# Attention weights copied into float32r tiles before they are transposed

## The chip, the cores and the metric

The kernel runs on one core of a Trainium2 chip. Its matmuls run on TensorE (PE in the profile; PEld is the same engine loading the stationary operand), the rest on VectorE (DVE), ScalarE (ACT) and GpSimd (POOL); SyncE (SP) issues most transfers. The metric is the device time of the run in microseconds; lower is better.

## The reference

One layer of a hybrid encoder, 1024 tokens by 1024 features, all in float32. The input is normalised and modulated, projected, and split over 16 heads of 64 features. Eight heads do softmax attention with a forget gate, eight do stick-breaking attention. Each head's output is gated, all are projected back, and a residual with a second normalisation ends the layer.

```python
# forgetting attention (8 heads)
s = einsum('bhqd,bhkd->bhqk', q, k) * scale + (f_q[..., :, None] - f_k[..., None, :])
p = softmax(where(causal, s, -inf));          out = einsum('bhqk,bhkd->bhqd', p, v)
# stick-breaking attention (8 heads)
log_keep = where(strict, log_sigmoid(-z), 0); later = cumsum(log_keep, reverse=True) - log_keep
w = where(strict, exp(log_sigmoid(z) + later), 0);  out = einsum('bhqk,bhkd->bhqd', w, v)
```

## The kernel before, in words

**Number formats.** float32r is TensorE's faster form of float32 with fewer mantissa bits. To keep precision, most operands are split into a rounded part (hi) and the rest (lo), both float32r, and a product is three matmuls (L312, L313, L314 for the projections). The transposes of the attention weights are different: they take the weights in plain float32 with a float32 identity.

**Units.** Heads go in pairs p = 0 to 7: pairs 0 to 3 are stick-breaking, 4 to 7 forgetting. A unit (p, h, i) is one block of 128 queries (i = 0 to 7) of head h of pair p; it sees ke = (i + 1) x 128 keys. There are 128 units, 16 to a pair. Pairs 1 to 3 run i upward, pairs 4 to 6 downward. Units are counted by k: pair 2 is k = 32 to 47, pair 4 is 64 to 79, pair 5 is 80 to 95, pair 6 is 96 to 111.

**A unit's steps.** att_scores: TensorE's scores (L483, L484) into PSUM. For stick-breaking, ACT's two sigmoids (L506, L508), DVE's scans (L514, L518) and POOL's product (L520) with its last column set to zero (L521) leave the weights in a tile be. For forgetting, DVE's addition and minimum (L491), ACT's exponential (L496), a reciprocal and POOL's scaling (L499) leave them in a tile a. Both come from one pool, att, of six tiles. att_transpose: i + 1 transposes of 128 x 128 (L537) into PSUM tiles T of up to four blocks, from each of which ACT writes the rounded part (L539) and DVE the rest (L540). A transpose is a matmul whose stationary operand is the block and whose moving operand is the identity. When both units of a pair of query blocks are transposed, att_pv multiplies by the values (L554).

**Order.** TensorE's order is written by hand: the loop at the end takes k = 0 to 130, and in each step issues the scores of unit k, the transposes of unit k - LAG (LAG = 2), and a share of the filling work from `fill`, which is the projections of later pairs, the values and the output. The other engines' and SP's orders are set by the scheduler, from the dependences and its own idea of times; each engine then runs its list strictly in order, so an instruction that waits holds all that follow on its engine.

**Value tiles.** The tag v is a pool of three 8 KB-per-partition buffers for the value tiles of a pair (two pairs are made at a time by make_v), and, at the two ends of the kernel, for the modulation's weights and for the last normalisation's gain and bias (load_ln, L905 and L906).

**Transfers.** SP issues the weight fetches (L123), whose results POOL splits (L125, L127, L128) into a ring of five tiles, the stores of gated outputs (L578), of scaled output weights (L896, L897), the copies of the keys from one half of the partitions to the other (L298), and the loads of the output weights (L886, L887). ACT issues the loads of the forget rows fb (L443).

Of the kernel before, what the change touches and what calls it, by code (L numbers as in the profile page):

```python
# [27 lines left out]
def tile_hybrid_layer(  # L28
# [55 lines left out]
    def after(*instructions):  # L84
        stack = ExitStack()
        for i in instructions:
            stack.enter_context(tc.issue_after(i.ins))
        return stack


    ident = cp.tile([P, P], F32, tag="ident", name="ident")
    make_identity(nc, ident)
    causal = cp.tile([P, P], F32, tag="causal", name="causal")
    nc.gpsimd.memset(causal, 0.0)
    nc.gpsimd.affine_select(out=causal, in_=causal, pattern=[[-1, P]], base=0,
                            channel_multiplier=1, compare_op=ALU.is_ge, fill=MASKED)
# [354 lines left out]
    def att_query(u):  # L451
# [3 lines left out]
        r = slice(h * HD, h * HD + HD)  # L455
        nc.scalar.copy(z[r, :], qst[p][h].bitcast(F32)[r, i * P:i * P + P])  # L456

    masks, scaled, lows, gates = [], [], [], []

    def att_causal(u):  # L460
# [9 lines left out]
    def att_scores(u, following):  # L470
        p, h, i = u
        z = zq.pop(u)
        ke = (i + 1) * P
        ns = 1 if ke <= 512 else 2
        w = ke // ns
        qs = slice(i * P, i * P + P)
        if p >= 4:
            f = fb[2 * (p - 4) + h]
        S = s_tile(f"S_{p}_{h}_{i}")
        halves = range(ns) if p >= 4 else range(ns)[::-1]  # L480
        for s in halves:
            ks = slice(s * w, s * w + w)
            nc.tensor.matmul(S[:, s, :w], qst[p][h][:, qs], kst[p][h][:, ks], start=True, stop=False)  # L483
            nc.tensor.matmul(S[:, s, :w], z, klo[p][:, ks], start=False, stop=True)  # L484
        v3 = lambda a: a[:, :ke].rearrange("p (a b) -> p a b", a=ns)
        if p >= 4:
            a = att_tile(f"a_{p}_{h}_{i}")
            nm = sb.tile([P, 1], F32, tag="nm", bufs=4, name=f"nm_{p}_{h}_{i}")
            l = sb.tile([P, 1], F32, tag="l", bufs=4, name=f"l_{p}_{h}_{i}")
            with after(*lows):  # L490
                nc.vector.tensor_tensor_reduce(out=v3(a), in0=S[:, :ns, :w], in1=v3(f),  # L491
                                               op0=ALU.add, op1=ALU.min, scale=-1.0, scalar=BIG,
                                               accum_out=nm)
            if following:
                att_causal(following)
            nc.scalar.activation(a[:, :ke], a[:, :ke], AF.Exp, scale=-1.0, bias=nm, accum_out=l)  # L496
            nc.vector.reciprocal(l, l)  # L497
            scaled[:] = [*scaled[-3:],
                         nc.gpsimd.tensor_scalar(a[:, :ke], a[:, :ke], l, 1.0, op0=ALU.mult, op1=ALU.mult)]  # L499
            st_w[u] = a  # L500
        else:
            kp = att_tile(f"kp_{p}_{h}_{i}")
            be = att_tile(f"be_{p}_{h}_{i}")
            with after(*key_casts):
                for s in halves:
                    nc.scalar.activation(kp[:, s * w:s * w + w], S[:, s, :w], AF.Sigmoid, scale=-1.0)  # L506
            key_casts.clear()
            last_act = nc.scalar.activation(v3(be), S[:, :ns, :w], AF.Sigmoid)  # L508
            gates[:] = [last_act]


            lo = ke - w
            rv = kp[:, lo:ke][:, ::-1]
            last_dve = nc.vector.tensor_tensor_scan(rv, rv, floor[:, :ke - lo], initial=0.0,  # L514
                                                    op0=ALU.mult, op1=ALU.max)
            if lo:
                rv = kp[:, :lo][:, ::-1]
                last_dve = nc.vector.tensor_tensor_scan(rv, rv, floor[:, P:P + 1].to_broadcast([P, lo]),  # L518
                                                        initial=kp[:, lo:lo + 1], op0=ALU.mult, op1=ALU.max)
            nc.gpsimd.tensor_tensor(be[:, :ke - 1], be[:, :ke - 1], kp[:, 1:ke], op=ALU.mult)  # L520
            nc.gpsimd.memset(be[:, ke - 1:ke], 0.0)  # L521
            st_w[u] = be
            return last_act, last_dve

    def att_transpose(u, between=()):
        p, h, i = u
        a = st_w.pop(u)
        j, qo = i // 2, (i % 2) * P
        for g in range((i // 4) + 1):
            n = min(4, i + 1 - 4 * g)  # L530
            if (p, h, j, g) not in st_pt:
                st_pt[p, h, j, g] = pt_tile(f"pt_{p}_{h}_{j}_{g}", F32R, [P, 2, 4, 256])
            hi, lo = (st_pt[p, h, j, g][:, x] for x in range(2))
            tp = t_tile(f"T_{p}_{h}_{i}_{g}")
            for b in range(n):
                kb = 4 * g + b
                nc.tensor.transpose(tp[:, b * P:(b + 1) * P], a[:, kb * P:(kb + 1) * P], ident)  # L537
            t3 = tp[:, :n * P].rearrange("p (a b) -> p a b", a=n)
            nc.scalar.copy(hi[:, :n, qo:qo + P], t3)  # L539
            lows[:] = [nc.vector.tensor_tensor(lo[:, :n, qo:qo + P], t3, hi.bitcast(F32)[:, :n, qo:qo + P],  # L540
                                               op=ALU.subtract)]
            while between:
                att_pv(*between.pop(0))
# [292 lines left out]
    for kb in range(NB):  # L836
# [9 lines left out]
        if kb < len(evacs):  # L846
            n, h = evacs[kb]
# [194 lines left out]
    FILL = (52, 72, 68, 68, 72, 72, 58, 16)  # L1042
    LEAD = 2
    LAG = 2
    W0 = 100.0
    OUT0 = 4
    TAIL = (2, 2, 2, 2, 2, 2, 4, 4, 4, 4, 8)
# [6 lines left out]
    def fill(want):  # L1054
        while done[0] < want:
            done[0] += 1
            next(fillers, None)
# [25 lines left out]
    tail = chain([gen_out_first(6), gen_out_last(6)] + [gen_out(t) for t in OUT_ORDER[1:]])  # L1083
    fill(4)
    def weights_turn(k):
        if LAG <= k < len(units) + LAG:
            u = units[k - LAG]
            att_transpose(u, ready)
            seen.add(u)
            if (u[0], u[1], u[2] ^ 1) in seen:  # L1090
                ready.append((u[0], u[1], u[2] // 2))
        while k >= len(units) + LAG and ready:
            att_pv(*ready.pop(0))

    def scores_turn(k):
        if k < len(units):
            if k == 16 * 4 - 1:
                load_fb(0)
                load_fb(1)
            if k == 0:  # L1100
                att_query(units[0])
            issued = att_scores(units[k], units[k + 1] if k + 1 < len(units) else None)
            if k == 16 * 4 - 1:
                att_causal(units[k + 1])
            if k in HELD:
                m, h = HELD[k]
                with after(*issued):
                    evac_m(0, m, 1, held[:, m * 512:(m + 1) * 512], (h,))
            with after(*(issued or ())):
                while summed:  # L1110
                    att_sum(*summed.pop(0))
            if k + 1 < len(units):
                att_query(units[k + 1])
            p, h, i = units[k]
            if 4 <= p < NPAIR - 1 and i == 0:
                load_fb(2 * (p - 4) + h + 2)

    for k in range(len(units) + LAG + 1):
        if k < 16 * 4:
            weights_turn(k)  # L1120
            scores_turn(k)
        else:
            scores_turn(k)
            fill(want[2 * k + LEAD + 1])
            weights_turn(k)
        fill(want[2 * k + LEAD + 2])
        if k >= LAST + OUT0:
            for _ in range(TAIL[min(k - LAST - OUT0, len(TAIL) - 1)]):
                next(tail, None)
        if k == LAST:  # L1130
# [69 lines left out]
```

## Time and profile before

| | |
|---|---|
| median of 3 runs | 680.5 us (680.24 to 680.56) |
| the profiled execution, first to last instruction (span; the page gives no other time for it) | 678.6 us |
| TensorE busy | 668.3 us, 98% |
| DVE, POOL, ACT busy | 72%, 60%, 56% |
| transposes of the weights (L537) | 576, 89.4 us of record time |
| transfers | 81.55 MB, mean 120 GB/s |

A row of the grouped view reads: line, engine, operation, what it writes and reads, shapes, count, then busy us and mean ns of one, then the idle time of the engine just before and what ended it. A matmul's duration goes from its start until its result is out, and neighbours overlap; what one costs TensorE is the distance from its start to the next one's. A row of the timeline starts with the start time and the duration in us; "x4" is four instructions in a row.

### The profile page before, as it was taken

Reading aid. Unit: us, or ns where it says so; the run is one execution under the profiler, and the core shown is the slowest. Engines: PE = TensorE matmul, PEld = TensorE weight load, DVE = VectorE, ACT = ScalarE, POOL = GpSimd, SP = SyncE. Lnnn points to the kernel's source line nnn. Section 1 sums busy time; section 2 is a strip of 40 time slices with the busy share of each in tenths; the row PEclk is TensorE's granted clock in tenths of the full one; section 3 lists DMA queues with packets and bytes.
Section 4 is the critical chain, followed back from the end, with each engine's and each line's share of the span. In section 5 each row is a group of like instructions: output and inputs, shape, how many; then the busy total and the mean of one; then the engine's idle time right before and its main releaser. Section 6 shows DMA issues by size and latency. Waiting matters only on the chain.

```text
span 678.6 us, 11231 instructions
## 1 busy us (share of the span) xinstructions
PE 668.3 (98%) x3713; PEld 571.2 (84%) x3713; DVE 485.9 (72%) x1001; ACT 382.6 (56%) x889; POOL 405.2 (60%) x530
## 2 busy tenths in 40 slices
PE   8999999999999999999999999999999999999995
PEld 4888898888998888889988888889988888888885
DVE  6787779868677777686776675766676777775645
ACT  5576468757567667576675564655565766521000
POOL 5560279755357556556378878785785365655412
PEclk9999999999999999999999999999999999999998
DMA  9983432112101112122124555263452297153301
GB/s 326 401 312 126 139 79 75 41 28 67 29 20 56 54 42 57 40 54 56 49 93 144 151 164 174 87 201 112 127 169 59 70 350 302 59 177 107 120 32 63
DMA packets 46474, 81.55 MB, mean 120 GB/s; under 512 B 5264, under 2 KB 20176, under 8 KB 46416
## 3 DMA queue, kind: packets, MB, share of 16 engines
q1 hardware_dynamic: 44832, 76.37, 35.1%
q10 hardware_dynamic: 1584, 4.47, 2.1%
q8 instruction: 29, 0.48, 0.3%
q14 instruction: 29, 0.24, 0.1%
HBM read 60.34 MB, written 16.29 MB: 113 GB/s over the span
## 4 chain that ended last, share of the span: by engine, by line
PE 97%; DMA 1%; DVE 0%; POOL 0%; ACT 0%; issue 0%; SPq 0%; POOLq 0%
PE m L312 11%; PE m L314 10%; PE m L313 10%; PE pv L554 10%; PE T L537 9%; PE S L484 5%; PE S L483 5%; PE o L939 4%; PE o L937 4%; PE o L938 4%; PE v L370 4%; PE v L372 4%; PE v L371 4%; PE st_q L647 1%; PE st_k L647 1%; PE st_late L647 1%
## 5 line engine op out<-in xcount | busy, mean ns | idle before, releaser
L540 DVE TENSOR_TENSOR pt<-T,pt 128x512 fp32r<-128x512 f32 (+2 forms) x192 | 102.7, 553 | 43.8 <-ACT pt L539 42.2
L539 ACT CAST pt<-T 128x512 fp32r<-128x512 f32 (+2 forms) x192 | 88.9, 479 | 64.5 <-PE T L537 62.5
L312 PE MATMUL m<-uh,whi 128*128 128x512 f32 x304 | 123.3, 405 | 0.1
L314 PE MATMUL m<-uh,wlo 128*128 128x512 f32 x304 | 119.8, 394 | 0.0
L313 PE MATMUL m<-ul,whi 128*128 128x512 f32 x304 | 119.7, 394 | 0.0
L520 POOL TENSOR_TENSOR be<-be,kp 128x127 f32<-128x127 f32 (+3 forms) x64 | 78.9, 1234 | 36.2 <-DVE kp L518 24.4
L554 PE MATMUL pv<-pt,v 128*128 128x512 f32 x320 | 82.8, 388 | 0.0
L514 DVE TENSOR_TENSOR_SCAN kp<-kp,floor 128x128 f32<-128x128 f32 (+3 forms) x64 | 58.6, 915 | 17.6 <-ACT kp L506 17.4
L499 POOL TENSOR_SCALAR a<-a,l 128x1024 f32<-128x1024 f32 (+3 forms) x64 | 48.4, 756 | 34.3 <-DVE l L497 26.0
L483 PE MATMUL S<-k,q 128*128 128x512 f32 (+5 forms) x192 | 68.8, 360 | 0.0
L314 PEld LDWEIGHTS m<-uh,wlo 128*128 128x128 f32 x304 | 57.1, 188 | 13.7
L496 ACT ACTIVATE a<-a,nm 128x1024 f32<-128x1024 f32 (+3 forms) x64 | 49.8, 779 | 28.6 <-DVE nm L491 28.1
L312 PEld LDWEIGHTS m<-uh,whi 128*128 128x128 f32 x304 | 57.2, 188 | 10.2 <-PE T L537 0.3
L484 PE MATMUL S<-kl,qz 128*128 128x512 f32 (+5 forms) x192 | 65.2, 341 | 0.0
L313 PEld LDWEIGHTS m<-ul,whi 128*128 128x128 f32 x304 | 57.3, 188 | 9.0
L554 PEld LDWEIGHTS pv<-pt,v 128*128 128x128 f32 x320 | 55.5, 189 | 8.9
L570 POOL TENSOR_TENSOR ty<-ty,sg 64x256 f32<-64x256 f32 x64 | 46.9, 733 | 23.4 <-issue 12.2
L491 DVE CUSTOM_DVE_ANT_0 a<-S,fb 128x1024 f32<-128x1024 f32 (+3 forms) x64 | 48.2, 753 | 16.9 <-PE S L484 12.0
L456 ACT CAST qz<-q 64x128 fp32r<-64x128 f32 x128 | 37.3, 296 | 34.2 <-PE S L484 33.0
L506 ACT ACTIVATE kp<-S 128x384 f32<-128x384 f32 (+4 forms) x96 | 44.0, 494 | 21.5 <-PE S L484 20.2
L370 PE MATMUL v<-whi_v,uh 128*128 128x256 f32 (+1 forms) x192 | 54.7, 285 | 0.0
L372 PE MATMUL v<-wlo_v,uh 128*128 128x256 f32 (+1 forms) x192 | 54.2, 282 | 0.0
(296 smaller groups left out, 1628.3 us busy)
## 6 DMA issues: line engine op xcount, KB each, us to landing
raw<-in_w_qkg_dram SPq DMA_DIRECT2D x38, 256.0 KB, 2.7
wss<-in_w_ss_dram SPq DMA_DIRECT2D x14, 512.0 KB, 8.1
x<-in_x_dram SPq DMA_DIRECT2D x8, 512.0 KB, 7.1
k<-k SPq DMA_DIRECT2D x32, 128.0 KB, 2.3
wg<-in_w_gate_dram SPq DMA_DIRECT2D x8, 512.0 KB, 4.9
raw_o<-in_w_out_dram SPq DMA_DIRECT2D x16, 256.0 KB, 3.0
fb<-f_dr ACTq DMA_DIRECT2D x8, 512.0 KB, 4.5
wo_dr<-whi_o SPq DMA_DIRECT2D x16, 256.0 KB, 2.1
```

What stands on the lines that cost most here:

```text
L312: nc.tensor.matmul(acc, hi[:, c], u_hi[kt][:, s], start=(kt == 0), stop=False)
L313: nc.tensor.matmul(acc, hi[:, c], u_lo[kt][:, s], start=False, stop=False)
L314: nc.tensor.matmul(acc, lo[:, c], u_hi[kt][:, s], start=False, stop=(kt == NB - 1))
L370: nc.tensor.matmul(acc[:, :n], u_hi[kt][:, ts_], hi[:, s], start=(kt == 0), stop=False)
L372: nc.tensor.matmul(acc[:, :n], u_hi[kt][:, ts_], lo[:, s], start=False, stop=(kt == NB - 1))
L483: nc.tensor.matmul(S[:, s, :w], qst[p][h][:, qs], kst[p][h][:, ks], start=True, stop=False)
L484: nc.tensor.matmul(S[:, s, :w], z, klo[p][:, ks], start=False, stop=True)
L520: nc.gpsimd.tensor_tensor(be[:, :ke - 1], be[:, :ke - 1], kp[:, 1:ke], op=ALU.mult)
L537: nc.tensor.transpose(tp[:, b * P:(b + 1) * P], a[:, kb * P:(kb + 1) * P], ident)
L539: nc.scalar.copy(hi[:, :n, qo:qo + P], t3)
L540: lows[:] = [nc.vector.tensor_tensor(lo[:, :n, qo:qo + P], t3, hi.bitcast(F32)[:, :n, qo:qo + P], op=ALU.subtract)]
L554: nc.tensor.matmul(acc2[:, :, q0:], vt[p][:, kb, h * P:(h + 1) * P], pt[:, :, q0:], start=(kb == 0), stop=(kb == last))
```

## The change

The identity is now a float32r tile with a float32 view of the same bytes. A new function hop, called when a unit's weights are ready, looks whether the unit's number lies in HOPS (35 to 47, 66 to 83, 98 to 111) and whether it has more than 256 keys. If so, it takes one half of a "room", a float32r tile of two times 1024 columns in the third buffer of the tag v (one room for each of the three ranges), and puts a transfer on a list that copies the weights there, byte for byte. The two halves are used in turn. send issues the listed transfers on SP: for pairs 0 to 3 one unit later than the unit's scores, just before the next unit's scores; for pairs 4 to 7 after the transposes that follow the unit's scores. att_transpose then transposes the copy as float32r, with the float32r identity, into the same PSUM tile. Units of other numbers go as before. The copied units are 35: eleven in pair 2, ten in pair 4, four in pair 5, ten in pair 6.

For units 32 to 48 (LATE) the transposes come three units after the scores and not two; at the end of the range two units are transposed in one step.

```diff
+    ident_r = cp.tile([P, P], F32R, tag="ident", name="ident")
+    ident = ident_r.bitcast(F32)
+    nc.gpsimd.memset(ident, 0.0)
+    nc.gpsimd.affine_select(out=ident_r, in_=ident, compare_op=ALU.not_equal, fill=1.0, base=0,
+                            pattern=[[-1, P]], channel_multiplier=1)
...
+    def hop(u, w, ke):
+        n = next((n for n, (a, b) in enumerate(HOPS) if a <= units.index(u) < b), None)
+        if n is None or ke <= 2 * P:
+            return w
+        if n not in room:
+            room[n] = sb.tile([P, 2, SEQ], F32R, tag="v", bufs=3, name=f"w_room_{n}")
+        hops[0] += 1
+        to = room[n][:, hops[0] % 2]
+        k = units.index(u)
+        late = u[0] < 4 or any(a <= k < b for a, b in LATE)
+        unsent.append((k + late, to.bitcast(F32)[:, :ke], w[:, :ke]))
+        return to
+
+    def send(k):
+        while unsent and unsent[0][0] <= k:
+            nc.sync.dma_start(*unsent.pop(0)[1:])
...
-            st_w[u] = a
+            st_w[u] = hop(u, a, ke)
...
-            st_w[u] = be
+            st_w[u] = hop(u, be, ke)
...
+        hopped = a.dtype == F32R
...
-                nc.tensor.transpose(tp[:, b * P:(b + 1) * P], a[:, kb * P:(kb + 1) * P], ident)
+                if hopped:
+                    nc.tensor.transpose(tp.bitcast(F32R)[:, b * P:(b + 1) * P], a[:, kb * P:(kb + 1) * P], ident_r)
+                else:
+                    nc.tensor.transpose(tp[:, b * P:(b + 1) * P], a[:, kb * P:(kb + 1) * P], ident)
...
+    HOPS = ((35, 48), (66, 84), (98, 112))
+    LATE = ((32, 49),)
...
-        if LAG <= k < len(units) + LAG:
-            u = units[k - LAG]
+        for n in (LAG + 1, LAG):
+            if not 0 <= k - n < len(units) or (n > LAG) != any(a <= k - n < b for a, b in LATE):
+                continue
+            u = units[k - n]
             att_transpose(u, ready)
...
             weights_turn(k)
+            send(k)
             scores_turn(k)
         else:
             scores_turn(k)
             fill(want[2 * k + LEAD + 1])
             weights_turn(k)
+            send(k)
```

Three places show the new order. The first is TensorE's list in pair 2, head 0, between two projection groups of pair 4's queries (fcum belongs to the forget gate). T_h_i_g is the PSUM tile of group g of unit i of head h, S its scores. Before, the unit ahead of the scores of i = 6 is i = 4, from its tile be:

```order
L427 MATMUL fcum<-flf,fscratch 128x64
L428 MATMUL fcum<-fsb,ones 128x64
L537 MATMUL T_0_4_0_2730<-ident,be_0_4_2652 128x128 x4
L554 MATMUL pv_0_1_2737<-pt_0_1_0_2636,v_1955 128x512 x3
L554 MATMUL pv_0_1_2737<-pt_0_1_0_2636,v_1955 128x2x128
L537 MATMUL T_0_4_1_2743<-ident,be_0_4_2652 128x128
L483 MATMUL S_0_6_2747<-k_0_1747,q_0_1564 128x448
```

Now, at the same place:

```order
L429 MATMUL fcum<-flf,fscratch 128x64
L430 MATMUL fcum<-fsb,ones 128x64
L563 MATMUL T_0_3_0_2725<-ident,w_room_2612 128x128 x4
L507 MATMUL S_0_6_2733<-k_0_1747,q_0_1564 128x448
L508 MATMUL S_0_6_2733<-kl_1749,qz_80 128x448
```

Unit i = 3 now stands ahead of the scores of i = 6, from the room; i = 4 and the multiplication by the values have moved behind one unit's filling work. In pairs 4 to 6 the order of the matmuls is as before.

The second is SP's list at the start of pair 5, whose first unit is (5, 0, 7). Before:

```order
L123 DMA raw_1_1_5111<-in_w_qkg_dram 128x512
L123 DMA raw_o_1_5117<-in_w_out_dram 128x512
L578 DMA y_dr<-ty_1_1_4952 64x256
L123 DMA raw_o_0_5240<-in_w_out_dram 128x512
L896 DMA wo_dr<-whi_o_1_5120 128x512
L897 DMA wo_dr<-wlo_o_1_5121 128x512
L123 DMA raw_v_0_5317<-in_w_v_dram 128x512
```

Now:

```order
L125 DMA raw_1_1_5138<-in_w_qkg_dram 128x512
L125 DMA raw_o_1_5144<-in_w_out_dram 128x512
L606 DMA y_dr<-ty_1_1_4975 64x256
L480 DMA w_room_4207<-a_0_7_4949 128x1024
L480 DMA w_room_4207<-a_0_6_4996 128x896
L125 DMA raw_o_0_5267<-in_w_out_dram 128x512
L924 DMA wo_dr<-whi_o_1_5147 128x512
L480 DMA w_room_4207<-a_0_5_5040 128x768
L925 DMA wo_dr<-wlo_o_1_5148 128x512
L125 DMA raw_v_0_5344<-in_w_v_dram 128x512
```

The copies stand between the fetches of weights and the stores, which keep their order among themselves.

The third is SP's list at the end of pair 6, where the loads of the last normalisation's gain and bias (lngb) now come, behind all copies and right ahead of the output weights (wol, woh):

```order
L480 DMA w_room_5981<-a_1_2_6475 128x384
L942 DMA yr_4_6652<-y_dr 128x3x128
L942 DMA yr_0_6937<-y_dr 128x4x128
L300 DMA k_0_6318<-k_0_6318 64x512
L977 DMA xr_7207<-in_x_dram 128x1024
L942 DMA yr_4_6943<-y_dr 128x3x128
L300 DMA k_1_6319<-k_1_6319 64x512
L933 DMA lngb<-in_ln_g_dram 128x1024
L934 DMA lngb<-in_ln_b_dram 128x1024
L915 DMA wol_6586<-wo_dr 128x1024
L914 DMA woh_6585<-wo_dr 128x1024
```

Before, the two loads stood among the weight fetches of pair 6's first units.

More of the change, by code (lines that the diff above doesn't have):

```diff
@@ L5 @@
 from concourse import mybir
-from concourse.masks import make_identity
 from concourse._compat import with_exitstack
@@ L88, in after @@
         return stack
-    ident = cp.tile([P, P], F32, tag="ident", name="ident")
-    make_identity(nc, ident)
+    ident_r = cp.tile([P, P], F32R, tag="ident", name="ident")
[3 more added lines that the diff above has]
+                            pattern=[[-1, P]], channel_multiplier=1)
     causal = cp.tile([P, P], F32, tag="causal", name="causal")
@@ L456, in att_query @@
         nc.scalar.copy(z[r, :], qst[p][h].bitcast(F32)[r, i * P:i * P + P])
+    hops = [0]
+    room, unsent = {}, []
+    def hop(u, w, ke):
[13 more added lines that the diff above has]
+            nc.sync.dma_start(*unsent.pop(0)[1:])
     masks, scaled, lows, gates = [], [], [], []
```

## Prediction

> **What bounds the kernel now.** I read the first and fourth parts of the page (busy time, the chain that ended last), then the waits of TensorE.
>
> ```profile
> span 678.6 us, 11231 instructions
> PE 668.3 (98%) x3713; PEld 571.2 (84%) x3713; DVE 485.9 (72%) x1001; ACT 382.6 (56%) x889; POOL 405.2 (60%) x530
> PE 97%; DMA 1%; DVE 0%; POOL 0%; ACT 0%; issue 0%; SPq 0%; POOLq 0%
> ...
> PE sc_all L179 <- POOL ident masks.py:199: 1.5, 1, 1.5
> PE xT_early L256 <- ACT x L222: 0.9, 1, 0.9
> PE st_q L647 <- ACT uh L270: 0.4, 1, 0.4
> ```
>
> The chain is TensorE for 97% of the span, and TensorE's listed waits come to 2.8 us, all in the start phase (x, modulation, first projection). So during attention a nanosecond taken out of TensorE's stream shortens the run by a nanosecond, and a wait put into it lengthens the run by as much. The other engines have room (DVE, the fullest, is busy 72%).
>
> **What a transpose costs.** The next rows are groups of TensorE's matmuls and weight loads (busy us, mean ns of one), then two stretches of its timeline (start, duration in us).
>
> ```profile
> L537 PE MATMUL T<-ident,be 128*128 128x128 f32 x288 | 44.7, 273 | 0.0
> L537 PE MATMUL T<-ident,a 128*128 128x128 f32 x288 | 44.7, 272 | 0.0
> L537 PEld LDWEIGHTS T<-ident,a x288: 137/140/143, 355.6 to 617.5; 128*128 128x128 f32 x144
> L434 PEld LDWEIGHTS frow<-ident,fc x1: 109/109/109, 234.9 to 234.9; 128*64 128x64 f32 x1
> L314 PEld LDWEIGHTS m<-uh,wlo 128*128 128x128 f32 x304 | 57.1, 188 | 13.7
> ...
> 405.16 0.40 PE L314 MATMUL m<-uh,wlo 128*128 128x512 f32 x1
> 405.39 0.71 PE L537 MATMUL T<-ident,a 128*128 128x128 f32 x5
> ...
> 377.34 0.22 PE L483 MATMUL S<-k,q 128*128 128x128 f32 x1
> 377.40 0.27 PE L484 MATMUL S<-kl,qz 128*128 128x128 f32 x1
> 377.51 0.45 PE L312 MATMUL m<-uh,whi 128*128 128x512 f32 x1
> 377.80 0.39 PE L313 MATMUL m<-ul,whi 128*128 128x512 f32 x1
> ```
>
> Five transposes last 0.71 us together, one 0.27: they follow each other every (0.71 - 0.27)/4 = 0.11 us. No float32r transpose stands in this trace. The nearest row is the 128-column score matmul, which is float32r: 0.22 us against 0.27, so its columns stream in 0.05 us less (about 0.055 against 0.11). But a transpose has its block as the stationary operand, so each needs a load, and a stream of 0.055 us helps only if the next load is as short. Loads first: in transposes 64 columns take 109 ns and 128 take 140, so 128 columns cost about 2 x 31 = 62 ns of loading (an estimate from these two rows) and the rest is latency. The projection's float32r loads take 188, 48 more, so about 110 ns of loading. The last four rows show what that does: from the first narrow matmul to the second wide one pass 377.80 - 377.34 = 0.46 us; a wide one streams in 405.39 - 405.16 = 0.23, so the narrow ones cost 0.115 each, though one streams in 0.055. They wait for loads.
>
> So two prices bound the new transpose. If its load is that of the float32 transpose (62 ns), it follows its neighbour after about 0.06 us and saves 0.05; if its load is that of a float32r matmul (110 ns), it saves nothing. I take the first: the plain float32 matmuls at the start also load in the long time (the row below, 190 ns), as float32r does, so the short load goes with the transpose and not with the number format, while the short stream goes with float32r.
>
> ```profile
> L185 PEld LDWEIGHTS sc_all<-ident,sc x16: 190/190/192, 6.1 to 8.1; 128*128 128x128 f32 x16
> ```
>
> The last transpose of a group is followed by a float32r matmul whose own long load can only begin with it, so that one keeps its 0.11 us. The Trainium skill, "TensorE: Matmul & The Clock Gate", section "LDWEIGHTS (loading the stationary operand)", has a load cost its columns over 1.2 GHz, 107 ns for 128, whatever the format; by that rule the sum of the next part would lose its gain entirely. The 188 and 190 ns rows fit the rule, the 140 and 109 ns rows of the transposes do not.
>
> **The change part by part.**
>
> *Transposes.* 35 units are copied; they have 191 of the 576 transposes, in 47 uninterrupted groups by the order. 191 - 47 = 144 transposes save 0.05 us: **-7.2 us**. If the last of each group saved too it would be 191 x 0.05 = 9.6.
>
> *Copies.* 35 transfers are added on SP's queue, 128 rows of 4 x ke bytes: 192 to 512 KB. The trace has no copy of this size from the on-chip memory to itself. Nearest rows (KB each, median us from issue to landing; the last row has the key copies' least, median and most):
>
> ```profile
> k<-k SPq DMA_DIRECT2D x32, 128.0 KB, 2.3
> fb<-f_dr ACTq DMA_DIRECT2D x8, 512.0 KB, 4.5
> wo_dr<-whi_o SPq DMA_DIRECT2D x16, 256.0 KB, 2.1
> xr<-in_x_dram SPq DMA_DIRECT2D x8, 512.0 KB, 3.5
> out_dram<-r SPq DMA_DIRECT2D x2, 512.0 KB, 2.8
> ...
> DMA to landing us min/median/max: 2.2/2.3/4.9
> ```
>
> 512 KB lies between 2.8 (a write) and 4.5 (a broadcast read). I take 3.3, near the plain read of 3.5, and 0.2 less for each 64 KB less, which gives 2.5 for 256 KB. What hides a copy is the time between the end of POOL's last write of the weights (L499 in pairs 4 to 7, L520 and L521 in pairs 0 to 3) and the unit's first transpose. A transpose whose copy is late holds all of TensorE, since everything behind it waits in its queue. I set the two ends beside each other for every copied unit. For most of pairs 4 to 6 there are 4 to 8 us. The thin ones, POOL's row first and TensorE's second:
>
> ```profile
> 242.85 2.00 POOL L520 TENSOR_TENSOR be<-be,kp 128x1023 f32<-128x1023 f32 x1 [1.52 <-DVE kp L518]
> 245.31 1.04 PE L537 MATMUL T<-ident,be 128*128 128x128 f32 x8
> 249.21 0.27 PE L537 MATMUL T<-ident,be 128*128 128x128 f32 x1
> 422.88 1.12 POOL L499 TENSOR_SCALAR a<-a,l 128x1024 f32<-128x1024 f32 x1
> 426.63 0.60 PE L537 MATMUL T<-ident,a 128*128 128x128 f32 x4
> 499.52 0.93 POOL L499 TENSOR_SCALAR a<-a,l 128x768 f32<-128x768 f32 x1
> 503.06 0.60 PE L537 MATMUL T<-ident,a 128*128 128x128 f32 x4
> 508.50 0.69 POOL L499 TENSOR_SCALAR a<-a,l 128x512 f32<-128x512 f32 x1
> 510.78 0.49 PE L537 MATMUL T<-ident,a 128*128 128x128 f32 x3
> 520.52 1.13 POOL L499 TENSOR_SCALAR a<-a,l 128x1024 f32<-128x1024 f32 x1 [0.36 <-DVE l L497]
> 525.03 0.60 PE L537 MATMUL T<-ident,a 128*128 128x128 f32 x4
> 525.88 1.02 POOL L499 TENSOR_SCALAR a<-a,l 128x896 f32<-128x896 f32 x1 [1.09 <-DVE l L497]
> 529.62 0.60 PE L537 MATMUL T<-ident,a 128*128 128x128 f32 x4
> ```
>
> Pair 2: the longest unit of head 0 (first three rows) leaves 0.46 us today, not enough for any copy. LATE moves its transposes to the next unit's place, 249.21, which leaves 4.4; the copy needs 3.3, and the two units before it are shortened by some 0.5: covered. Without LATE TensorE would wait about 3 us there.
>
> Pairs 5 and 6 keep LAG = 2. Each deficit is copy + 0.1 for the hand-over + what the transposes of the two units before it save - the space. Unit (5,0,7): 3.3 + 0.1 + 0 - 2.6 = 0.8. Unit (6,0,5): 2.9 + 0.1 + 0 - 2.6 = 0.4. Unit (6,0,3): 2.5 + 0.1 + 0.4 - 1.6 = 1.4, but part of its lateness goes (next). Unit (6,1,7): 3.3 + 0.1 - 3.4 = 0. Unit (6,1,6): 3.1 + 0.1 + 0.3 - 2.7 = 0.8.
>
> *The normalisation's gain and bias.* Their two 512 KB loads now wait for the buffer that the third room holds, and move behind pair 6's copies. Today they are issued at 496.3 us, and POOL then waits for a weight transfer that shared the engines with them:
>
> ```profile
> L905 SPq DMA_DIRECT2D lngb<-in_ln_g_dram x1: 525/525/525, 496.3 to 496.3; - x1
> ...
> 504.55 0.62 POOL L127 TENSOR_SCALAR whi<-raw 128x512 fp32r<-128x512 f32 x1 [1.12 <-DMA raw<-in_w_qkg_dram]
> ```
>
> That 1.1 us stands ahead of unit (6,0,3)'s scaling, whose deficit so falls to about 0.2 (0.3 rounding up). Later they go out just ahead of the output weights' 16 loads; the first output matmuls read only two of the eight pairs, and I take the rest to have room: 0.
>
> *Other SP work.* Each copy waits on SP for POOL (and for the transposes of the unit two before, which used the same half); weight fetches, y stores and key copies queue behind it. They wait for the same POOL stream today and stand in POOL's order beside the copies, so I cost this at 0; if that cover is gone, a fetch a few us late meets the ring of five weight tiles, which hides it.
>
> *Order.* In pair 2 ACT's and DVE's evacuations move by one unit with the transposes; nothing is added to them. POOL's identity is built by the same two instructions.
>
> **Sum:** -7.2 + 0.8 + 0.4 + 0.3 + 0 + 0.8 = **-4.9 us**. The profiled span of 678.6 becomes 673.7. The median of the runs, 680.5, is 1.9 above the span; the same 1.9 gives **675.6 us**.
>
> **The rivals.**
>
> *A, copies never late* (each lands within the space): the whole 7.2 stays, 673.3. For it: the writes above take 2.1 to 2.8 us, and a unit that is late gives the next one room. Against it: 1.6 to 2.7 us of space at four units.
>
> *B, the load sets the pace* (110 ns, as for float32r matmuls): no transpose gets faster, TensorE streams as today, and the late copies are pure loss: 0.8 + 0.4 + 0.5 (unit (6,1,6), now without the shortening) = 1.7, so 682.2, slower. It decides at one row: the float32r transpose's load at 188 instead of 140. For it: every float32r load of the trace has 188. Against it: the float32 matmuls have 190 too. This is the case in which the skill's rule above holds.
>
> *C, slow copies*: on-chip copies of 512 KB run like the 4.5 us broadcast, 1.2 us more each. Then the five thin units pay up to 2.0 + 1.6 + 1.5 + 1.2 + 2.0, and the next thinnest about 2 together: 10.3 against 7.2, so 683.6. The turn is at about 0.6 us over my price. For it: with other transfers in flight even the 128 KB key copies reach 4.9. Against it: their median is 2.3.
>
> **How the numbers follow.** Forecast 52%, A 24%, B 16%, C 8%. Runs of this kernel agree within 0.3 us, and I call up to 0.2% (1.4 us) no change. The forecast's own range is 673 to 679; nearly all of it and all of A is faster. Between the cases (half the gain eaten by waits) lies some "same". Faster 0.74, same 0.07, slower 0.19. The range starts below A, for the case that the groups' last transposes also gain, and ends between the forecast's edge and B: 672 to 681.5.
>
> **What would show it.** Float32r transposes spaced 0.06 us, loads near 140 ns: step one holds; spaced 0.11 us: B. Copies of 512 KB landing after about 3.3 us, and TensorE waits on them at (5,0,7), (6,0,5), (6,1,6) of under 1 us each and none in pair 2. Waits at many units, or a 512 KB copy over 4 us, would be C. The forecast is wrong as a whole if TensorE's share of the chain falls well below 97%.

## The result, and the profile after

The changed kernel takes 682.93 us (median of 10 runs, 680.29 to 684.04) against 680.45 (10 runs, 680.07 to 680.56) for the kernel before: a ratio of 1.0032, 95% interval 1.0022 to 1.0041. It is slower by 0.3%, where 675.6 was predicted. Its runs also spread over 3.7 us, those of the kernel before over 0.5. The execution whose profile follows is the slowest of the ten (684.04, span 682.2); three more executions come below.

First the head of the page of the changed kernel and its chain of waits, to be read beside the three rows of the prediction's first fence:

```profile
span 682.2 us, 11348 instructions
...
PE 667.3 (98%) x3713; PEld 567.7 (83%) x3713; DVE 485.9 (71%) x1001; ACT 382.0 (56%) x889; POOL 405.1 (59%) x530
...
PE 86%; DMA 6%; DVE 3%; POOL 2%; ACT 1%; issue 1%; SPq 0%; POOLq 0%; DVEq 0%; ACTq 0%
```

TensorE was 97% of the chain and is 86%: transfers, DVE and POOL now stand in it. Its waits (what waited, for what: us in total, times, longest):

```profile
PE S L507 <- DVE nm L515: 1.7, 1, 1.7
...
PE T L563 <- DMA w_room<-a: 1.0, 2, 0.6
PE v L374 <- POOL wlo_v L130: 0.9, 1, 0.9
PE m L314 <- DVE kl L301: 0.7, 1, 0.7
PE st_q L675 <- ACT uh L272: 0.6, 1, 0.6
PE pv L582 <- DVE ty L597: 0.5, 1, 0.5
PE T L563 <- DVE fb L492: 0.2, 1, 0.2
PE v L372 <- POOL whi_v L129: 0.2, 1, 0.2
```

Before, all listed waits lay in the start phase. Now two rows belong to the copies: w_room, and the transposes at 408.0 us that the view puts down to DVE (T <- DVE fb), whose copy landed at 407.87. Of the others, the longest is a score matmul that waits for DVE, then the value weights (wlo_v, whi_v), the evacuation of pair 7's keys (kl) and of a gated output (ty). The view counts a wait from where the pipeline has run dry; measured as the distance between the ends of neighbouring matmuls over the usual one (the median of the same pair of lines and shapes), the stalls come to 10.6 us in this execution against 3.1 before (sum of all above 25 ns), and that is how waits are given from here on. From 40 us on, behind the start phase, they are 8.9 against 1.7.

The new transposes, in the view of their line (least, median, most ns):

```profile
L563 PEld LDWEIGHTS T<-ident,w_room x191: 137/140/197, 230.6 to 545.6; 128*128 128x128 f32 x191
L563 PE MATMUL T<-ident,w_room x191: 221/246/282, 230.7 to 545.6; 128*128 128x128 f32 x191
```

and the copies, in the view of theirs:

```profile
DMA to landing us min/median/max: 2.1/2.9/4.8
```

The load is 140 ns as before and the matmul's record is shorter (246 against 272): rival B, a load of 188, is out. But the spacing is not 0.06. Two rows of the changed kernel's timeline (start, duration):

```profile
395.54 0.70 PE L563 MATMUL T<-ident,w_room 128*128 128x128 f32 x7
...
400.84 0.28 PE L563 MATMUL T<-ident,w_room 128*128 128x128 f32 x2
```

Two take 0.28 where one takes 0.22: the second follows after 0.06. Seven take 0.70, so six steps of (0.70 - 0.22)/6 = 0.08 on average. By the ends of all 144 neighbours (medians), the first step of a group is 64 ns and each later one 85, where it was 109; the loads from a group's second one on also start 85 ns apart. And a matmul of 512 columns behind a group ends 302 ns after the last transpose, where it was 233. A group of n transposes with the matmul behind it took 109n + 233 and takes 61 + 64 + 85(n - 2) + 302, that is 24(n - 1) ns less. Over 47 groups with 191 transposes this is 24 x 144 = **3.5 us**, half of the 7.2 that was predicted.

### The profile page after: what moved, and what is told of

It is laid out like the page before. It is cut to its first block, busy times and chain, and to the rows that moved or that the text cites. A ratio compares the mean times of both kernels' runs of the same rounds, so it can differ in the third digit from the quotient of the medians.

```text
span 682.2 us, 11348 instructions
## 1 busy us (share of the span) xinstructions
PE 667.3 (98%) x3713; PEld 567.7 (83%) x3713; DVE 485.9 (71%) x1001; ACT 382.0 (56%) x889; POOL 405.1 (59%) x530
## 4 chain that ended last, share of the span: by engine, by line
PE 86%; DMA 6%; DVE 3%; POOL 2%; ACT 1%; issue 1%; SPq 0%; POOLq 0%; DVEq 0%; ACTq 0%
PE pv L582 9%; PE m L314 8%; PE m L316 8%; PE m L315 8%; PE T L565 6%; PE S L507 5%; PE S L508 4%; PE o L966 4%; PE o L965 4%; PE o L967 4%; PE v L374 4%; PE v L372 4%; PE v L373 4%; PE T L563 2%; DMA fb<-f_dr 1%; PE st_q L675 1%
```

## The experiments

Each time is the median of the runs, with the kernel before on the same chip beside it. "The format" is float32r against float32 for the transposes.

### What the format is worth

e1 transposes the copies as plain float32 and leaves all else:

```diff
-nc.tensor.transpose(tp.bitcast(F32R)[:, ...], a[:, ...], ident_r)
+nc.tensor.transpose(tp[:, ...], a.bitcast(F32)[:, ...], ident)
```

> All 35 copies stay, but the copies are transposed as plain float32, with the float32 view of the identity, so only the format of 191 transposes goes back. Theory S (small gain, many waits): in the trace of the changed kernel the float32r transposes follow each other every 82 ns in the middle of a group and the matmul behind a group comes later, which makes about 17 ns saved per transpose, 3.3 us in all. Then this kernel takes 682.9 + 3.3 = 686.2 us (685.4 to 687.2). Theory P (the predicted price, 7.2 us gained, and more lost elsewhere than I see): 682.9 + 7.2 = 690.1. Theory N (the format gains nothing at all): 682.9.

Measured: 683.27 (682.68 to 684.08; before 680.21; ratio 1.0044, 1.0032 to 1.0057). Neither S's number nor P's; N's 682.9 is nearest. Going back to plain float32 costs only 0.3 us against the changed kernel (0.8 by the ratios, whose intervals overlap), although every transpose is back at 109 ns. It is no clean comparison, though. The scheduler goes by its own idea of times, and with the other format it set the lists of SP, POOL and DVE differently: the fetch of the value weights went out two us earlier and its wait was gone. Stalls were 5.9 us here, 10.6 in the first execution of the changed kernel. So copies and order in these lists, without any gain from the format, cost 3.1 us, and in the median execution of the changed kernel the format's 3.5 us are nearly all used up by waits. Fastest run against fastest (680.29 and 682.68), 2.4 of the 3.5 are left.

The cleaner pair came later: e9 and e10 copy only 18 units, where copies have room (their edit is told below), e9 with the format and e10 without. TensorE's order is the same in both. The other lists are nearly so: four of SP's 312 transfers and five of POOL's 531 instructions stand elsewhere, against 17 and 18 between e1 and the changed kernel.

> The same kernel as the one without the last copies, with its 95 copied transposes as plain float32. Theory S: 95 x 17 ns = 1.6 us more than that kernel, so 680.6 if it takes 679.0. Theory P (0.05 us each but for the last of a group): 3.5 more. Theory N (the waits take what the format gives, whatever is copied): the same time.

Measured: e10 681.01 (680.74 to 681.53; before 680.29), e9 679.59: the format is worth 1.4 us for 95 transposes in 24 groups (1.1 by the means; only two of e9's eleven runs reach e10's fastest). 24 ns x 71 is 1.7, the prediction's 50 ns would be 3.5. Theory S holds, P falls, and N too: where few copies are late (in e9 one by 0.6 us and one by 0.2), most of the gain reaches the end. The same stretch of both timelines, e10 first, then e9:

```profile
391.88 0.60 PE L563 MATMUL T<-ident,w_room 128*128 128x128 f32 x4
392.24 0.60 PE L582 MATMUL pv<-pt,v 128*128 128x512 f32 x2
392.68 0.60 PE L563 MATMUL T<-ident,w_room 128*128 128x128 f32 x4
393.03 0.48 PE L314 MATMUL m<-uh,whi 128*128 128x512 f32 x1
393.35 0.40 PE L315 MATMUL m<-ul,whi 128*128 128x512 f32 x1
```

```profile
391.11 0.45 PE L563 MATMUL T<-ident,w_room 128*128 128x128 f32 x4
391.39 0.59 PE L582 MATMUL pv<-pt,v 128*128 128x512 f32 x2
391.82 0.46 PE L563 MATMUL T<-ident,w_room 128*128 128x128 f32 x4
392.11 0.47 PE L314 MATMUL m<-uh,whi 128*128 128x512 f32 x1
392.42 0.39 PE L315 MATMUL m<-ul,whi 128*128 128x512 f32 x1
```

From the first row's start to the last row's: 1.47 us and 1.31, 0.16 less for two groups of four (24 x 6 = 0.14).

### Pair 2 and its late order

e6 makes no copies at all and keeps only LATE:

```diff
-    HOPS = ((35, 48), (66, 84), (98, 112))
+    HOPS = ()
```

> No copies at all: the kernel before, but pair 2's transposes come three units after the scores, with two units in one step at the end of the range. Theory S: the multiplication by the values that follows those two units waits 0.8 us for DVE at 290 us, since DVE has the evacuations of two units to do there, and two smaller waits of 0.2 come with the order: 680.2 + 0.8 to 1.2 = 681.2 (680.9 to 681.5). Theory P (the order costs nothing): 680.2.

Measured: 681.37 (before 680.37; ratio 1.0017, 1.0008 to 1.0026). The order costs 1.0 us, as S said. Its row among TensorE's waits:

```profile
PE pv L582 <- DVE ty L597: 0.6, 1, 0.6
```

At the end of the range two units are transposed in one step, and the product with the values behind them finds DVE still evacuating (0.87 us by the ends of the matmuls, at 291 us).

e4 takes pair 2's copies and the late order out of the changed kernel:

```diff
-    HOPS = ((35, 48), (66, 84), (98, 112))
-    LATE = ((32, 49),)
+    HOPS = ((66, 84), (98, 112))
+    LATE = ()
```

> No copies in pair 2, and its transposes come two units after the scores as before. Theory S: over pair 2 the transposes stood 0.48 us ahead of the kernel before at the start and 0.48 at its end; 63 transposes gain 1.1 us and three waits (0.8 at the end of the range, where two units come in one step, 0.2 and 0.2) eat them. So the time is the same: 682.9 (682.4 to 683.4). Theory P: 44 transposes of 0.05 us are lost, 682.9 + 2.2 = 685.1.

Measured: 682.37 (680.70 to 684.00; before 680.21; ratio 1.0029, 1.0016 to 1.0043). The interval overlaps the changed kernel's. S's range is missed by 0.03. Pair 2's 63 copied transposes bring no more than their order costs; P's 2.2 us are not there.

### Pair 5

e3 ends the second range four units earlier:

```diff
-    HOPS = ((35, 48), (66, 84), (98, 112))
+    HOPS = ((35, 48), (66, 80), (98, 112))
```

> The second range ends at unit 79 and not 83: the four copies at the start of pair 5 go. Theory S: the first of them came 0.8 us late, and with them SP's order around the fetch of the value weights of pairs 6 and 7 changed, for which TensorE waited 1.5 us at 454 us. Gone are 2.3 us of waits and about 0.4 of gain (26 transposes of 17 ns): 682.9 - 1.9 = 681.0 (680.4 to 681.7). Rival V (the value weights are late because the whole kernel fetches later, not because of these four): only the 0.8 goes, 682.9 - 0.8 + 0.4 = 682.5, and the wait at 454 us stays.

Measured: 679.92 (679.33 to 680.79; before 680.21; ratio 0.9997, 0.9988 to 1.0006). This is 3.0 us less than the changed kernel by the medians (2.4 by the ratios), and as fast as the one before; more than S expected. Both waits, for the copy of (5,0,7) and for the value weights, are gone. How these four copies reach the value weights is in POOL's timeline. The changed kernel, then the kernel before (the bracket is the idle time ahead and what ended it):

```profile
447.29 0.62 POOL L129 TENSOR_SCALAR whi_v<-raw_v 128x512 fp32r<-128x512 f32 x1 [3.33 <-DMA raw_v<-in_w_v_dram]
...
453.19 0.62 POOL L129 TENSOR_SCALAR whi_v<-raw_v 128x512 fp32r<-128x512 f32 x1 [0.98 <-DMA raw_v<-in_w_v_dram]
```

```profile
443.87 0.62 POOL L127 TENSOR_SCALAR whi_v<-raw_v 128x512 fp32r<-128x512 f32 x1 [0.89 <-DMA raw_v<-in_w_v_dram]
...
449.15 0.61 POOL L127 TENSOR_SCALAR whi_v<-raw_v 128x512 fp32r<-128x512 f32 x1
```

The last quarter of the value weights is split 4.0 us later (453.19 against 449.15), because the second fetch is issued at 444.28 and not at 440.87, and the two behind it follow some 3 us late: in the new list of SP it stands behind a key copy and behind a store of output weights that POOL now makes later and whose issue takes 1.50 us there (0.32 before). In e3 it goes out at 439.74. In e1 and e11 (below) the four copies are there and it goes out at 442.15 and 441.38, without a wait at TensorE. So it is the order into which the scheduler put POOL's and SP's work around the copies, and not the load of the copies.

### The end of pair 6: forget row and keys

The longest wait of the changed kernel is not its own copy's. DVE adds the causal mask to pair 7's forget row (fb), whose transfer came late; the score matmul at 555.56 needs DVE's next minimum:

```profile
552.97 0.29 DVE L492 TENSOR_TENSOR fb<-fb,causal_ps 128x128 f32<-128x128 f32 x1 [1.96 <-DMA fb<-f_dr]
```

The row took 8.6 us to land; before, 5.7. It had no room before either: it landed at 549.44, and DVE's addition began at 549.54. The change moved the two loads of gain and bias right beside it, so I first took them for the cause. e2 holds them back by a small write of POOL into their tile:

```diff
-    def load_ln():
+    def load_ln(w):
         lgb[0] = sb.tile([P, 2, D], F32, tag="v", bufs=3, name="lngb")
+        nc.gpsimd.tensor_scalar(lgb[0][:, :, 0:1], w[:, None, 0:1].to_broadcast([P, 2, 1]), 1.0, 1.0, op0=ALU.mult, op1=ALU.mult)
...
-        if k == LAST:
-            load_ln()
+        if k == LAST + 4:
+            load_ln(st_w[units[k]])
```

> The two loads of the last normalisation's gain and bias are held back until unit 116 of 128 is scaled (by a write of POOL into their tile), so that they go out behind the output weights and not ahead of them, beside the forget row of pair 7. Theory S: these 1 MB of broadcast loads delay the forget row, for which DVE and then TensorE waited 1.95 us at 555.6 us. Then the forget row lands in about 5.8 us again (8.6 in the changed kernel, 5.7 before) and the time falls by 1.9, to 681.0 (680.4 to 681.6). Rival D (the transfers of that stretch in general, since the output weights now take the place of the two loads in the queue): the forget row still takes over 8 us, time 682.9.

Measured: 681.59 (680.47 to 682.96; before 680.21; ratio 1.0020, 1.0010 to 1.0030), the forget row in 5.8 us and no wait for it. That looked like S. But e5 and e8 hold the loads back too:

```diff
-    HOPS = ((35, 48), (66, 84), (98, 112))
-    LATE = ((32, 49),)
+    HOPS = ((66, 80), (98, 112))
+    LATE = ()
```

This is e5; in e8 only (98, 112) stands in HOPS.

> Only pair 4 (units 66 to 79) and pair 6 (98 to 111) are copied, 20 units with 102 transposes; pair 2 has its old order, and the gain and bias loads are held back until unit 116 is scaled. Theory S: from the kernel without pair 5's copies (679.9) the waits at the end of pair 2's late order (0.8 and 0.4) and the last of the gain-and-bias wait (0.2) go, and pair 2's gain of 1.1 goes: 679.6 (679.0 to 680.2), a tie with the kernel before (680.2) or just under it. Theory P (0.05 us for each transpose that is not the last of a group): pairs 4 and 6 gain 3.8, less some 1.0 of late copies: 677.4.

> Only pair 6's ten units (98 to 111, 51 transposes) are copied, pair 2 in its old order, the gain and bias loads held back until unit 116 is scaled. Theory S: 0.9 us gained, 0.4 lost at two late copies, 0.5 at the copy of pair 7's keys, which shares the transfer engines with the last copies: 680.2 (679.7 to 680.8). Theory P: 1.9 gained, 1.2 lost at the copies (0.4, 0 and 0.8): 679.5.

Measured: e5 680.07 (before 680.37; ratio 0.9994, 0.9985 to 1.0003), within S's range and far from P's 677.4; e8 681.23 (ratio 1.0013, 1.0004 to 1.0022), above both. In both the forget row was late again, 7.3 and 8.1 us, and TensorE waited 0.7 and 1.5 us for it, with the two loads far behind. So the row is late without the gain and bias loads beside it, and e2's number came out without showing S's cause. What e5 and e8 share with the changed kernel is pair 6's last copies, just ahead of the loads of gated outputs and of pair 7's keys. e9 leaves out two of them:

```diff
-    HOPS = ((66, 80), (98, 112))
+    HOPS = ((66, 80), (98, 108))
```

> As the kernel with pairs 4 and 6 alone (680.1), but without the last two copies of pair 6, units (6,1,3) and (6,1,2). Theory S2 (in place of the gain and bias loads, which were held back in the two kernels that still waited for the forget row): the last copies stand in SP's queue ahead of the loads of gated outputs in rows of 512 bytes, and push them and the copy of pair 7's keys against the forget row. Then the forget row lands in 5.2 to 5.8 us (7.3 to 8.6 with the copies), the key copy in 2.3 (3.2), their waits of 0.7 and 0.6 go, 7 transposes of 17 ns are lost: 680.1 - 1.1 = 679.0 (678.5 to 679.6). Rival R (any copy in pair 6 does it, or chance): the forget row takes over 6.5 us, 680.1.

Measured: 679.59 (679.23 to 681.08; before 680.29; ratio 0.9995, 0.9987 to 1.0004). The forget row lands in 5.4 us, the key copy in 2.3 (2.8 in the changed kernel), and the two waits are gone, as S2 said. Against e5 only 0.5 of the expected 1.1 us came off by the medians, and nothing by the ratios.

The wait at the keys has another cause than S2's. TensorE waits there for DVE's evacuation of the keys (kl, whose matmul is m), not for the key copy. DVE's list in the kernel before, then in the changed one:

```profile
544.04 0.43 DVE L568 TENSOR_TENSOR ty<-pv,ty 64x256 f32<-64x256 f32 x1
544.39 0.69 DVE L299 TENSOR_TENSOR kl<-m,k 64x512 fp32r<-64x512 f32 x1
545.00 0.42 DVE L569 TENSOR_TENSOR ty<-pv,ty 64x256 f32<-64x256 f32 x1
```

```profile
544.90 0.43 DVE L596 TENSOR_TENSOR ty<-pv,ty 64x256 f32<-64x256 f32 x1
545.36 0.43 DVE L597 TENSOR_TENSOR ty<-pv,ty 64x256 f32<-64x256 f32 x1
545.71 0.69 DVE L301 TENSOR_TENSOR kl<-m,k 64x512 fp32r<-64x512 f32 x1
```

The scheduler put the evacuation behind both additions of a gated output (ty). In the nine executions with that order TensorE waits 0.84 to 0.87 us here, in the eight with the old one 0.27 to 0.29. The eight include e1 and e11, which make pair 6's last copies and whose key copy takes 2.7 us. So this wait comes with the new lists and not with the load of the copies.

### The load of the copies by itself

e11 makes the 24 copies of pairs 4 to 6, which nobody reads; the weights are transposed from their own tiles:

```diff
-            st_w[u] = hop(u, a, ke)
+            st_w[u] = a
+            hop(u, a, ke)
```

> The 24 copies of pairs 4, 5 and 6 are made but nobody reads them: the weights are transposed from their own tiles as plain float32 (pair 2 has no copies and its old order, the gain and bias loads are held back). No transpose can wait for a copy here, so what is left is what the transfers and the changed order do to others. Theory S2: the copy of pair 7's keys and the forget row still wait, 0.3 to 0.6 and 0.7 to 1.5: 680.3 + 1.0 to 2.1 = 681.8 (681.2 to 682.4); no wait for the value weights at 454 us, because the second fetch stands ahead of the key copies again. Rival L (copies cost only by their own lateness): 680.3.

Measured: 680.67 (680.36 to 681.13; before 680.29; ratio 1.0006, 0.9997 to 1.0015). All copies run, the forget row takes 5.8 us, and TensorE waits for nothing that it did not wait for before; its list holds the start phase only. S2's 1.0 us or more did not come; L's "nothing" is within the interval. In its profiled execution the units' scores start 0.53 us late at pair 2, ahead of all copies, and 0.51 at the last unit, so nothing was lost beside the copies.

e7 copies pair 4 alone:

```diff
-    HOPS = ((35, 48), (66, 84), (98, 112))
-    LATE = ((32, 49),)
+    HOPS = ((66, 80),)
+    LATE = ()
```

> Only pair 4's ten units (66 to 79, 51 transposes) are copied, pair 2 in its old order. Theory S: 51 x 17 ns = 0.9 us gained, at most 0.2 lost to late copies: 680.2 - 0.8 = 679.4 (679.0 to 680.0). Theory P: 51 transposes in 13 groups, 38 x 0.05 = 1.9 gained: 678.3. Rival T (each gain comes back as waits, whatever is copied): 680.2.

Measured: 680.01 (679.25 to 681.43; before 680.37; ratio 0.9996, 0.9987 to 1.0005). The median is 0.4 lower, half of S's 0.8 and far from P's 678.3; the interval includes no change. In its profiled execution (679.25, the fastest of the eleven) pair 4 gains 0.90 us, as the spacing gives (24 ns x 38).

### The same kernel again, and the best one

> The changed kernel again, for another profiled execution. Theory S (structure): the wait at the end of the late order (0.8), the key copy's (0.8) and the copies' own (about 2) stand in every execution, since each follows from the order of the instructions. Theory Z (chance): the forget row's wait (1.95 in the first profile) and the value weights' (1.6) lie anywhere from 0.2 to 2 and make the spread, so that an execution with span X has its two waits smaller by 682.2 - X than the first profile's 3.5 together.

The same was expected of the other two, e12b and e12c. Their times are 682.49, 680.42 and 680.65. The stalls (us) of the four executions of the changed kernel, with the time the forget row took to land:

| | first | e12a | e12b | e12c |
|---|---|---|---|---|
| span | 682.2 | 680.7 | 678.6 | 678.9 |
| forget row lands in | 8.6 | 7.9 | 5.3 | 5.3 |
| wait for the forget row | 1.95 | 1.24 | 0 | 0 |
| wait for the value weights | 1.58 | 0.53 | 0.52 | 0.68 |
| copy (5,0,7) | 0.84 | 0.82 | 0.44 | 0.33 |
| copy (6,0,5) | 0.61 | 0.16 | 0.07 | 0.12 |
| key evacuation | 0.84 | 0.87 | 0.86 | 0.86 |
| end of the late order | 0.78 | 0.78 | 0.79 | 0.79 |
| all stalls | 10.6 | 7.8 | 6.7 | 6.6 |
| stalls from 40 us on | 8.9 | 6.8 | 4.9 | 5.0 |

Both theories hold in part. The key evacuation and the end of the late order stand in every execution, and so do some 0.5 us at the value weights, which Z had put down to chance. The forget row, the rest of the value weights' wait and, against S, the copies' lateness make the spread. The read of the input issued beside the forget row (xr, 512 KB) came late with it: 8.5 and 8.0 us in the first two executions, 4.1 in the other two. And the loads of gain and bias lie beside the forget row in all four, so e12b and e12c settle that they do not delay it by themselves. The row's transfer in e12b, in the view of transfers (KB, us from issue to landing):

```profile
fb<-f_dr ACTq DMA_DIRECT2D x1, 512.0 KB, 5.3
```

e13 leaves out one more copy, of unit (6,0,5), for which TensorE waited 0.6 us in e9:

```diff
-    HOPS = ((66, 80), (98, 108))
+    HOPS = ((66, 80), (99, 108))
```

> As the kernel without the last copies of pair 6 (679.6), and without the copy of unit (6,0,5), for which TensorE waited 0.6 us there. Theory S: 0.6 us of wait and 6 transposes of 17 ns go: 679.6 - 0.5 = 679.1 (678.7 to 679.7), 0.2% under the kernel before (680.3). Rival: the next copy, of unit (6,0,4), is as late in its place, and the time stays at 679.6.

Measured: 680.01 (679.26 to 680.50; before 680.42; ratio 0.9992, 0.9983 to 1.0001). Not faster than e9: the rival's time holds, though the late copies are others than it said (0.4 us at unit (6,0,3), 0.34 and 0.25 in pair 4). e9 and e13 have the lowest medians against the kernel before, by 0.7 and 0.4 us, but the interval of neither excludes no change.

### Where the time went, unit by unit

The start of a unit's scores in an execution, less its start in the kernel before (us; negative is earlier), at the start of each pair, at the last unit, and for the span:

```
                  pair 2  pair 4  pair 5  pair 6  pair 7  last   span
changed, first     -0.46   -0.48   -1.03    0.87    1.33   3.22   3.67
changed, e12a      -0.03    0.01   -0.49    0.34    0.50   1.66   2.13
changed, e12b       0.00   -0.05   -0.78   -0.34   -0.27  -0.40   0.06
e9 (format)        -0.45   -0.46   -1.41   -1.41   -1.39  -1.42  -1.35
e10 (plain)        -0.05   -0.04   -0.03   -0.03    0.43   0.42   0.79
e6 (order only)    -0.36    0.83    0.83    0.83    0.84   0.85   0.79
```

Pair 2 nets nothing in the changed kernel. Pair 4 gains 0.95 us where nothing is late (e9), 0.5 to 0.7 in the changed kernel. Pair 5 gives back 0.4 to 1.9. Pair 6 gains nothing in any: in e9 late copies take 0.8 us there. Pair 7 costs up to 1.9, and in another execution of the same kernel nothing. The rest lies behind the last unit: in the changed kernel some 0.4 us pass between the last store's landing and the end of the span beyond what passed before; why is open.

## Why the prediction was wrong, step by step

**A transpose gains 0.05 us: half of it.** That the load stays at 140 ns was right, and so was the step of 0.06, but only for the second transpose of a group. From the third on the step is 85 ns, and what the format saves there is 24 ns. I estimated the loading from two durations (31 ns per 64 columns) and took a group to run at that pace throughout; a steady stream of load and matmul runs slower than its first pair, one load every 85 ns where I had counted 62. The term is 3.5 us, not 7.2 (by the spacing; e9 and e10 measured 1.4 where the spacing gives 1.7). Of the steps that failed this is the largest: 3.7 of the 7.3 us between the forecast and the measured time. The Trainium skill, "TensorE: Matmul & The Clock Gate", section "Back-to-back issue gap", gives about 81 ns for each of a sustained stream of loads and matmuls of 128 columns, and 56 as the gap of a matmul by itself. The traces' 85 and 64 lie 4 and 8 ns above that. I had weighed only the load rule of the same page, by which there would be no gain; e9 and e10 show that there is one.

**The last transpose of a group saves nothing: right.** The matmul behind it waits for its own load: it ends some 500 ns after that load began in both kernels (medians 504 and 501), and the load began 2 ns after the last transpose before and 49 now. The group's sum is 24(n - 1).

**Copies land after 3.3 us for 512 KB, 2.5 for 256: right in size, but not in the slope.** In the first execution the 512 KB copies took 2.8 to 3.0 us and those of 256 KB 2.3 to 3.7, in the median 3.1; the size hardly matters, and the median over all is 2.9. **Their lateness of 2.3 us in sum: right in sum, not in place.** (5,0,7) waited 0.84 (0.8 predicted), (6,0,5) 0.61 (0.4), (6,1,6) 0.24 (0.8), (6,0,3) none (0.3), (4,1,3) 0.39 (none predicted): 2.1 in the first execution, about half of that in the fastest.

**The late order of pair 2 costs 0: wrong, 1.0 us** (e6). I counted the evacuations and found none added, but two units' worth meet in one step at the end of the range, ahead of what the values' product needs.

**Other SP work costs 0, its cover being the ring of five: wrong.** The cover did not hold for the value weights, which are needed a few us after they are fetched. What I missed is that the change also moved POOL's and SP's order around pair 5. Waits of 0.5 to 1.6 us; with the copy of (5,0,7), pair 5's copies cost 2.4 to 3.0 us (e3), of which the traces account for some 2; where the rest went is open.

**The gain and bias loads cost 0: nothing here speaks against it.** With the loads held back the forget row was late all the same (e5, e8), and with them in place it came in time (e12b, e12c). But the work beside them was not free: the forget row took 5.3 to 8.6 us in the eleven executions that have pair 6's last copies (seven of them over 6.5), and 4.8 to 5.7 in the six that do not. This count speaks for the last copies taking part. It does not prove it, and e9 against e5 cannot, being one execution each. Why the same kernel has the row at 5.3 once and at 8.6 another time is open, since all lists are the same in both.

**DVE's order outside pair 2: not in the sum, so put at 0 without a reason.** The new order on DVE at pair 7's keys costs 0.6 us beyond the 0.3 waited before, in every execution.

**"A nanosecond taken out of TensorE's stream shortens the run by a nanosecond": right only while nobody else is close.** With the whole change in place, the format's 3.5 us came back as waits for DVE, POOL and transfers in the median execution (e1, with other lists on SP and POOL, is 0.3 to 0.8 us slower and not 3.5). With 18 copies in roomy places 1.4 of 1.7 stayed (e9, e10). The prediction had named its own sign of being wrong as a whole, TensorE's share of the chain well below 97%: it is 86%.

Of the rivals, A and C fall with the measured copies. C (683.6) and B (682.2) ended nearest to the time, both by luck: C's slow copies are not there, and B's price is not, since the load is 140 ns and follows every 85, not 110. The sum as measured in the execution e12a: -3.5 (format) + 1.2 (late order with its two small waits at 215 and 276 us) + 1.8 (copies) + 0.5 (value weights) + 0.6 (key evacuation beyond the 0.3 it waited before) + 1.2 (forget row) + 0.4 (behind the last store) = +2.2; its span less that of the kernel before is 2.1.

## What to carry to other kernels

A kernel whose chain is 97% one engine can have others close behind it (here a transfer that landed 0.1 us before it was needed): before a saving of 1% is counted, look for what is finished only just in time. Price a short instruction by the steady spacing in a long group and not by its first pair. And where a scheduler sets the other queues' order, an edit that adds transfers also moves work that it does not name: compare the lists of every engine around each place where something is fetched shortly before it is used.

## What was not expected of the hardware

- A float32r transpose of 128 x 128 follows its predecessor after 64 ns once, then every 85 ns (the changed kernel, e9); plain float32 109 throughout (the kernel before, e10). The load's record is 140 ns in both.
- A copy from the on-chip memory to itself of 192 to 512 KB lands 2.1 to 4.8 us after its issue, median 2.9 (the changed kernel's first execution). With 24 of them that nobody read the median was 0.4 us higher (interval 0.2 lower to 1.0 higher), and the trace shows no loss beside them (e11).
- A broadcast load of 512 KB (the forget row) with other transfers in flight landed in 5.3 to 8.6 us in executions of one and the same kernel. Kernels in which TensorE ran on float32r copies spread over 1.2 to 3.7 us between runs, e10 and e11 (plain) over 0.8, e1 (plain, with all copies) over 1.4. What makes the spread beyond the forget row stays open.
